# Decoder trunk on one core: convolution input kept in SBUF, attention loads moved to SP's queue, norm factors spread by PE transposes

## The chip, the cores and the metric

One core of a Trainium2 chip runs the whole program: two layers of a decoder trunk over 1024 tokens. The metric is device microseconds of one execution, the median of three runs. Matmuls run on TensorE (PE), element-wise work on VectorE (DVE), ScalarE (ACT) and GpSimd (POOL); SyncE (SP) only issues DMAs. POOL can issue DMAs too, on a queue of its own.

## The reference

```python
for i in range(DEPTH):                               # 2 layers, S = 1024 tokens, D_MODEL = 1024
    a = rmsnorm(h, norm_mix_pre[i])
    u = a @ w_in[i]                                   # q, k, v, qi, ki, wi, u_conv (512), u_pool (256)
    # partial rope on q, k, qi, ki
    y_attn = dsa_sparse_attention(q, k, v, qi, ki, wi)
    #   per block of 128 queries: index score of every causal key (16 heads), top 256 keys,
    #   softmax attention (8 heads of 64, 2 kv heads) over these keys alone
    y_conv = conformer_conv(u_conv, ...)
    #   y = a * sigmoid(g); causal depthwise conv, 31 taps; + bias; LayerNorm over 256; swish; 256x256
    y_pool = multiscale_pool(u_pool, ...)             # trailing means of 2/4/8/16, 64x64 maps, scale
    h = h + rmsnorm(concat(y_attn, y_conv, y_pool) @ w_out[i], norm_mix_post[i])
    m = square(relu(rmsnorm(h, norm_mlp_pre[i]) @ w_up[i])) @ w_down[i]       # d_ff = 4096
    h = h + rmsnorm(m, norm_mlp_post[i])
    h = h + sigmoid(h @ ple_gate[i]) * (p[i] @ ple_proj[i])
```

## The kernel before

Activations lie transposed: channels on the 128 lanes, tokens in the free dimension. Each layer is done in two halves of 512 tokens. The eight phases of `PHASES` alternate `win` (norm and the 21 units of the input projection) and `m` (output projection, MLP, gate) of (layer, half): win(0,0), win(0,1), m(0,0), win(1,0), m(0,1), win(1,1), m(1,0), m(1,1). A *unit* is one 128-channel output tile: 8 pieces of weights, each used in three 128x512 matmuls (lines 243, 248, 249) on a high and a low part of weights and activations.

**Weights** (`prepare`, line 196): SP loads 512 KB into one of two `wraw` buffers (line 199), ACT copies the high part into `whi` (line 204), POOL makes the low part `wlo` (line 205). `whi` and `wlo` have four tiles, two units' worth, so PE frees what ACT needs next.

**Background.** Convolution and pooling (`conv_pool`) and attention (`attention`) are Python generators. After every unit of a phase, `run` advances them by a share that `RATES` gives to the phase. A generator that has begun stays ahead of an attention that is inserted later (line 429). From the program so recorded a scheduler makes one fixed order for each engine's queue.

**Convolution input.** In `win_phase` the units A0, G0, A1, G1 give the gated input: DVE evacuates A into a `dtmp` tile (line 342), G is scaled, passes a tanh on ACT and is multiplied in (line 391); SP stores the tile to `cpS` in DRAM (line 392), as it does for the pooling input P0, P1 (line 397). `conv_pool` loads both back with their left context into `row` tiles (`window`, lines 475 and 477). Then DVE makes the 2 x 31 taps, one instruction each (lines 535 and 537), into a PSUM bank. The pooling has POOL adds (499 to 503), DVE means (508 to 510), a split (261) and three matmuls on `cmat`.

**Norm factors.** `token_sums` (line 298) makes sums over the lanes by matmuls with a column of ones; `rms` raises them to the power -1/2 on POOL (line 311); `spread` (line 303) copies four columns of factors over the lanes as four fp32 matmuls with `ident` as moving operand. This happens 16 times in `rms_sb` and `post_norm`, and in every `conv_pool` twice, for the mean (`mu`) and for the variance.

**Attention.** POOL issues the loads of keys `kd` (line 613), values `vst` (line 836), queries `qst` (line 608) and, at the start of an `m` phase, of the mixed heads `slot<-mixS` (line 923). The choice of 256 keys (`select`) is a search bit by bit: 31 rounds, in each of which ACT counts two blocks (line 683) and DVE two (line 669), with throw-away flags in tiles of the ring that is `spare`; in the second half of a layer that is the ring `row`, of which two tiles hold the packed scores. Buffers: `dtmp` 11, `row` 5 tiles.

## Time and profile before

| | us |
|---|---|
| median of 3 runs | 2843.78 (2837.95 to 2844.03) |
| profiled execution, own time | 2843.85 |
| its span, first to last instruction | 2842.1 |
| PE busy | 2720.5 (96%) |
| PE weight loads busy | 2242.8 (79%) |
| DVE busy | 1747.6 (61%) |
| ACT busy | 1548.1 (54%) |
| POOL busy | 1418.0 (50%) |
| granted TensorE clock, mean | 0.985 |

Busy time is the union of instruction times. Matmuls overlap: a 128x512 matmul is shown 0.39 us long, while the next one starts 0.23 us after it, so what a matmul costs is read from the distance of starts and not from its length. The profile's rows give start, length, engine, line, tiles and, in brackets, the idle time of the engine before and what ended it.

### The profile page before, as it was taken

Reading aid. Unit: us, or ns where it says so; the run is one execution under the profiler, and the core shown is the slowest. Engines: PE = TensorE matmul, PEld = TensorE weight load, DVE = VectorE, ACT = ScalarE, POOL = GpSimd, SP = SyncE. Lnnn points to the kernel's source line nnn. Section 1 sums busy time; section 2 is a strip of 40 time slices with the busy share of each in tenths; the row PEclk is TensorE's granted clock in tenths of the full one; section 3 lists DMA queues with packets and bytes.
Section 4 is the critical chain, followed back from the end, with each engine's and each line's share of the span. In section 5 each row is a group of like instructions: output and inputs, shape, how many; then the busy total and the mean of one; then the engine's idle time right before and its main releaser. Section 6 shows DMA issues by size and latency. Waiting matters only on the chain.

```text
span 2842.1 us, 37724 instructions
## 1 busy us (share of the span) xinstructions
PE 2720.5 (96%) x12648; PEld 2242.8 (79%) x12648; DVE 1747.6 (61%) x3473; ACT 1548.1 (54%) x2932; POOL 1418.0 (50%) x1161
## 2 busy tenths in 40 slices
PE   7899989999999999899999989999999999999998
PEld 6677777887888878778788777888878878788886
DVE  7969679788447775965822467587985561511123
ACT  5347667775567535766334423677757654533343
POOL 4655425444334665544544755444443356544446
PEclk9999999999999999999999999999999999999999
DMA  5676554422343576533333547534223354423233
GB/s 189 198 192 218 153 134 148 112 85 90 93 115 106 159 238 187 162 116 102 114 104 104 184 152 238 152 116 108 97 79 98 104 164 138 155 97 99 98 97 122
DMA packets 195666, 384.90 MB, mean 135 GB/s; under 512 B 17424, under 2 KB 76944, under 8 KB 195472
## 3 DMA queue, kind: packets, MB, share of 16 engines
q1 hardware_dynamic: 138192, 330.58, 35.7%
q0 software_dynamic: 57280, 51.91, 8.7%
q8 instruction: 100, 1.64, 0.3%
q14 instruction: 94, 0.77, 0.1%
HBM read 307.97 MB, written 74.45 MB: 135 GB/s over the span
## 4 chain that ended last, share of the span: by engine, by line
PE 72%; DVE 16%; DMA 5%; ACT 3%; issue 3%; POOL 1%; SPq 0%; POOLq 0%; DVEq 0%; ACTq 0%
PE pd L243 20%; PE pd L249 20%; PE pd L248 20%; PE bank L601 5%; DVE bank L537 2%; PE bank L789 2%; DVE dtmp L875 1%; DVE row L669 1%; DVE slot L261 1%; DMA row<-cpS 1%; PE bank L798 1%; PE bank L797 1%; DVE cmat L261 1%; PE pd L298 1%; DVE dtmp L261 1%
## 5 line engine op out<-in xcount | busy, mean ns | idle before, releaser
L205 POOL TENSOR_TENSOR wlo<-wraw,whi 128x512 fp32r<-128x512 f32 x824 | 1094.7, 1334 | 1180.6 <-ACT whi L204 1115.4
L243 PE MATMUL pd<-slot,whi 128*128 128x512 f32 x3296 | 1306.8, 397 | 50.7 <-DVE slot L261 14.5
L248 PE MATMUL pd<-slot,whi 128*128 128x512 f32 x3168 | 1246.0, 393 | 4.6 <-DVE slot L261 2.7
L249 PE MATMUL pd<-slot,wlo 128*128 128x512 f32 x3168 | 1241.9, 393 | 4.1 <-POOL wlo L205 4.0
L204 ACT ACTIVATE whi<-wraw 128x512 fp32r<-128x512 f32 x824 | 511.1, 627 | 731.3 <-PE pd L248 499.0
L243 PEld LDWEIGHTS pd<-slot,whi 128*128 128x128 f32 x3296 | 625.6, 190 | 188.4 <-DVE slot L261 16.6
L249 PEld LDWEIGHTS pd<-slot,wlo 128*128 128x128 f32 x3168 | 600.0, 189 | 130.9 <-POOL wlo L205 7.5
L248 PEld LDWEIGHTS pd<-slot,whi 128*128 128x128 f32 x3168 | 601.1, 190 | 125.8 <-DVE slot L266 3.9
L601 PE MATMUL bank<-kd,qst 128*128 128x512 f32 (+3 forms) x1024 | 261.5, 360 | 10.6 <-DVE mxc L767 3.7
L646 DVE SCALAR_TENSOR_TENSOR idx<-bank,wiT,idx 128x512 f32<-128x512 f32 (+3 forms) x300 | 189.3, 652 | 94.7 <-ACT bank L642 90.7
L601 PEld LDWEIGHTS bank<-kd,qst 128*128 128x128 f32 x1024 | 181.7, 192 | 46.6 <-DVE idx L646 6.8
L642 ACT ACTIVATE bank<-bank 128x512 f32<-128x512 f32 (+2 forms) x320 | 153.8, 506 | 90.0 <-PE bank L601 85.2
L981 DVE SCALAR_TENSOR_TENSOR pd<-pd,rb 128x512 f32<-128x512 f32 x112 | 77.7, 694 | 183.2 <-PE pd L249 183.2
L995 DVE TENSOR_TENSOR yT<-yT,pd 128x512 f32<-128x512 f32 x96 | 65.5, 684 | 197.8 <-PE pd L249 197.5
L537 DVE SCALAR_TENSOR_TENSOR bank<-row,vec,bank 128x512 f32<-128x512 f32 x232 | 162.1, 746 | 0.5
L669 DVE TENSOR_SCALAR_CACHE_REDUCE row<-row,cc 128x640 f32<-128x640 uint16 (+1 forms) x124 | 133.5, 1077 | 14.5 <-ACT row L683 12.6
L683 ACT ACTIVATE row<-row,cc 128x768 f32<-128x768 uint16 (+1 forms) x124 | 121.5, 983 | 18.0 <-DVE cc L689 15.3
L767 DVE CUSTOM_DVE_ANT_0 row<-bank,idx 128x512 f32<-128x512 f32 (+3 forms) x160 | 91.4, 591 | 64.0 <-PE bank L601 60.6
L261 DVE TENSOR_TENSOR cmat<-bank,cmat 128x512 fp32r<-128x512 f32 (+1 forms) x160 | 97.9, 631 | 49.4 <-ACT cmat L260 43.8
L261 DVE TENSOR_TENSOR slot<-pd,slot 128x512 fp32r<-128x512 f32 x112 | 76.6, 685 | 51.3 <-ACT slot L260 51.1
L982 ACT ACTIVATE pd<-pd 128x512 f32<-128x512 f32 x112 | 65.2, 582 | 72.8 <-DVE pd L981 72.7
L775 ACT ACTIVATE row<-row,nmc 128x384 f32<-128x384 f32 (+5 forms) x96 | 84.2, 878 | 27.8 <-DVE nmc L771 21.0
(216 smaller groups left out, 2828.7 us busy)
## 6 DMA issues: line engine op xcount, KB each, us to landing
wraw<-wup SPq DMA_DIRECT2D x128, 512.0 KB, 3.3
wraw<-wdown SPq DMA_DIRECT2D x128, 512.0 KB, 3.3
wraw<-win SPq DMA_DIRECT2D x84, 512.0 KB, 4.2
qiS<-dtmp SPq DMA_DIRECT2D x64, 256.0 KB, 2.5
slot<-mixS POOLq DMA_DIRECT2D x32, 512.0 KB, 7.0
wraw<-wgate SPq DMA_DIRECT2D x32, 512.0 KB, 3.6
qst<-qiS POOLq DMA_DIRECT2D x48, 256.0 KB, 3.7
hS<-yT SPq DMA_DIRECT2D x48, 256.0 KB, 3.6
```

What stands on the lines that cost most here:

```text
L204: sc.activation(hi, r, AF.Copy)
L205: gp.tensor_tensor(lo, r, hi.bitcast(F32), op=OP.subtract)
L243: te.matmul(ps, wh, xh, start=i == 0, stop=False)
L248: te.matmul(ps, wh, xl, start=False, stop=False)
L249: te.matmul(ps, wl, xh, start=False, stop=i == n - 1)
L261: ve.tensor_tensor(lo, src, hi.bitcast(F32), op=OP.subtract)
L537: ve.scalar_tensor_tensor(acc[:, c] if k == TAPS - 1 else pa, src, w, pa, op0=OP.mult, op1=OP.add)
L601: te.matmul(ps[:, :n1 - n0], q, kd[:, k, k0 + n0:k0 + n1], start=k == 0, stop=k == 1)
L642: sc.activation(r, r, AF.Relu)
L646: ve.scalar_tensor_tensor(at, r, w, at, op0=OP.mult, op1=OP.add)
L669: ve.tensor_scalar(flags[:, :Ws[j]], of[j], t, None, op0=op, op1=OP.add, accum_out=dst[:, j:j + 1])
L683: sc.activation(flags[:, :Ws[j]], of[j], AF.Sign, scale=-1.0, bias=c[:, j:j + 1], accum_out=cnt[:, j:j + 1])
```

## The change

- The gated convolution input is written into a tile of a new ring `win` (2 tiles of 2 x 542 columns, 30 of them left context). The context is zero in a layer's first half and is copied on ACT from the kept tile `halo` in the second. The store to `cpS`, the load back and two `dtmp` tiles per phase go; the pooling input still passes through DRAM (`plS`).
- Loads of `kd`, `vst` and `slot<-mixS` (16 pairs, 12 and 32 DMAs) are issued by SP instead of POOL. Those of `qst` stay on POOL.
- `spread` uses `te.transpose` instead of an fp32 matmul. The mean of the convolution's LayerNorm is one fp32 matmul with a 128x128 matrix of 1/256 in place of `token_sums`, a scaling and a `spread`.
- Rings: `dtmp` 11 to 9, `row` 5 to 4. Three of the eight `RATES` change.

```diff
-RATES = (1.171, 1.114, 0.558, 0.766, 0.722, 0.567, 0.741, 0.946)
+RATES = (1.205, 1.114, 0.558, 0.766, 0.751, 0.567, 0.731, 0.946)
...
-    dtmp = Ring("dtmp", 11, [P, HALF])
+    dtmp = Ring("dtmp", 9, [P, HALF])
...
-    rows = Ring("row", 5, [P, 1088])
+    rows = Ring("row", 4, [P, 1088])
+
+    wins = Ring("win", 2, [P, 2, TAPS - 1 + HALF])
+    halo = const.tile([P, 2, TAPS - 1], F32, name="halo")
...
-            te.matmul(ps[:, j * P:(j + 1) * P], t4[:, j:j + 1].to_broadcast([P, P]), ident, start=True, stop=True)
+            te.transpose(ps[:, j * P:(j + 1) * P], t4[:, j:j + 1].to_broadcast([P, P]), ident)
...
-                conv[name[1]] = evac(ps, half=True)
+                c = int(name[1])
+                if c == 0:
+                    yc = wins.get()
+                    if hf == 0:
+                        gp.memset(yc[:, :, :TAPS - 1], 0.0)
+                    else:
+                        sc.activation(yc[:, :, :TAPS - 1], halo, AF.Copy)
+                ve.scalar_tensor_tensor(yc[:, c, TAPS - 1:], ps, 0.5, rb, op0=OP.mult, op1=OP.mult)
...
-                y = conv[name[1]]
+                y = yc[:, c, TAPS - 1:]
                 ve.scalar_tensor_tensor(y, g, 1.0, y, op0=OP.add, op1=OP.mult)
-                sy.dma_start(cpS[l, c * P:(c + 1) * P, ts], y)
-                dtmp.put(y)
+                if c == 1 and hf == 0:
+
+                    sc.activation(halo, yc[:, :, HALF:], AF.Copy)
...
-        yt, yc = window(0, TAPS - 1)
...
-        token_sums(ps, [both])
+        te.matmul(ps, mean256, both, start=True, stop=True)
         ctmp.put(both)
-        mu = tiny("mu")
-        ve.tensor_scalar(mu, ps[:, :4], 1.0 / 256, None, op0=OP.mult)
-        spread(ps, mu)
...
-                gp.dma_start(kd[dup * 64:(dup + 1) * 64, :, k0:k0 + n],
+                sy.dma_start(kd[dup * 64:(dup + 1) * 64, :, k0:k0 + n].bitcast(F32),
...
-                            gp.dma_start(vst[:, v0:v0 + n // P], vS[l, bkv, :, :n // P])
+                            sy.dma_start(vst[:, v0:v0 + n // P].bitcast(F32), vS[l, bkv, :, :n // P])
...
-            gp.dma_start(xs[k], mixS[:, k * P:(k + 1) * P, ts].rearrange("k p t -> p k t"))
+            sy.dma_start(xs[k].bitcast(F32), mixS[:, k * P:(k + 1) * P, ts].rearrange("k p t -> p k t"))
```

The order of every queue moves with this. Line numbers of the changed kernel are 4 to 10 higher. First, DVE's queue in win(0,0), before. L535 and L537 are taps, `row_127` is the window loaded from `cpS`, L344 evacuates the pooling input P0 and then P1, L391 finishes G1:

```order
L349 TENSOR_TENSOR pd_138<-pd_138,rb_163 128x512
L391 SCALAR_TENSOR_TENSOR dtmp_107<-pd_138,dtmp_107 128x512
L344 TENSOR_TENSOR dtmp_103<-pd_139,rb_163 128x512
L535 TENSOR_SCALAR bank_142<-row_127,vec 128x512
L535 TENSOR_SCALAR bank_143<-row_127,vec 128x512
L537 SCALAR_TENSOR_TENSOR bank_142<-row_127,vec,bank_142 128x512
L344 TENSOR_TENSOR dtmp_104<-pd_137,rb_163 128x512
```

DVE's queue at the same place in the changed kernel; L401 finishes G0 and L395 begins A1, L545 and L547 are taps, L189 to L193 are rope tables:

```order
L401 SCALAR_TENSOR_TENSOR win_125<-pd_139,win_125 128x512
L190 TENSOR_SCALAR dtmp_104<-dtmp_101 128x512
L545 TENSOR_SCALAR bank_142<-win_125,vec 128x512
L191 TENSOR_SCALAR dtmp_104<-dtmp_104 128x512
L189 TENSOR_SCALAR dtmp_103<-dtmp_109,fr 128x512
L547 SCALAR_TENSOR_TENSOR bank_142<-win_125,vec,bank_142 128x512
L193 SCALAR_TENSOR_TENSOR dtmp_101<-dtmp_104,dtmp_101 128x512
L395 SCALAR_TENSOR_TENSOR win_125<-pd_137,rb_164 128x512
L547 SCALAR_TENSOR_TENSOR bank_142<-win_125,vec,bank_142 128x512
```

The first tap moves from behind G1 and P0 to right behind G0, and P1's evacuation has one load less in front of it that DVE must wait for.

Second, DVE's queue in a round of `select` of (0,1), before: L669 counts a block (640 and 1024 columns), its first name is the tile for the flags:

```order
L689 SCALAR_TENSOR_TENSOR cc_1427<-gec_1431,bank_141 128x4
L669 TENSOR_SCALAR row_125,cntc_1387<-row_126,cc_1427 128x640
L687 TENSOR_SCALAR bank_141<-cc_1427 128x4
L669 TENSOR_SCALAR row_127,cntc_1387<-row_124,cc_1427 128x1024
L688 TENSOR_TENSOR gec_1432<-cntc_1387,bank_141 128x4
L689 SCALAR_TENSOR_TENSOR cc_1428<-gec_1432,bank_141 128x4
L669 TENSOR_SCALAR row_127,cntc_1384<-row_126,cc_1428 128x640
```

The same in the changed kernel, where L676 counts:

```order
L696 SCALAR_TENSOR_TENSOR cc_1413<-gec_1421,bank_141 128x4
L694 TENSOR_SCALAR bank_141<-cc_1413 128x4
L676 TENSOR_SCALAR row_121,cntc_1373<-row_124,cc_1413 128x640
L676 TENSOR_SCALAR row_123,cntc_1373<-row_122,cc_1413 128x1024
L988 SCALAR_TENSOR_TENSOR pd_137<-pd_137,rb_164 128x512
L695 TENSOR_TENSOR gec_1418<-cntc_1373,bank_141 128x4
L696 SCALAR_TENSOR_TENSOR cc_1414<-gec_1418,bank_141 128x4
L694 TENSOR_SCALAR bank_141<-cc_1414 128x4
L676 TENSOR_SCALAR row_121,cntc_1374<-row_124,cc_1414 128x640
```

Two flag tiles (121 and 123) take the place of three (123, 125, 127), and an evacuation (L988) stands in the round.

Third, SP's queue in the changed kernel at the start of m(0,0); L819 stores a finished attention block, L620 and L843 load keys and values for the next half, L930 loads the mixed heads, L206 loads weights:

```order
L620 DMA kd<-kS 64x2x1024 x2
L819 DMA mixS<-ctmp_113 64x4x128
L819 DMA mixS<-ctmp_110 64x4x128
L843 DMA vst<-vS 128x1024
L819 DMA mixS<-ctmp_110 64x4x128
L819 DMA mixS<-ctmp_112 64x4x128
L930 DMA slot_75<-mixS 128x2x512
L930 DMA slot_76<-mixS 128x2x512
L930 DMA slot_77<-mixS 128x2x512
L930 DMA slot_78<-mixS 128x2x512
L206 DMA wraw_91<-wout 128x512
```

Before, SP's queue had only stores and weight loads here, and the four kinds of loads stood on POOL's.

## Rows read from the trace of the kernel before

**Rows 1.** The page, part 1: busy time and share of each engine.

```profile
PE 2720.5 (96%) x12648; PEld 2242.8 (79%) x12648; DVE 1747.6 (61%) x3473; ACT 1548.1 (54%) x2932; POOL 1418.0 (50%) x1161
```

**Rows 2.** Timeline of PE at 208: start, length, line, tiles, count.

```profile
208.46 0.39 PE L249 MATMUL pd<-slot,wlo 128*128 128x512 f32 x1
208.69 1.05 PE L303 MATMUL bank<-ident,muc 128*128 128x128 f32 x8
209.50 0.48 PE L243 MATMUL pd<-slot,whi 128*128 128x512 f32 x1
209.81 0.39 PE L248 MATMUL pd<-slot,whi 128*128 128x512 f32 x1
```

**Rows 3.** Timeline of PE at 741: twelve transposes of attention, line 789.

```profile
740.96 1.47 PE L789 MATMUL bank<-ident,row 128*128 128x128 f32 x12
742.19 0.48 PE L243 MATMUL pd<-slot,whi 128*128 128x512 f32 x1
```

**Rows 4.** Groups by line: PE's small norm matmuls of `conv_pool`.

```profile
L298 PE MATMUL bank<-ones,ctmp 128*128 128x1 f32 x64 | 7.6, 239 | 0.0
L303 PE MATMUL bank<-ident,muc 128*128 128x128 f32 x32 | 4.2, 274 | 0.0
```

**Rows 5.** Timeline of PE: the first matmuls on loaded `mixS`, m(0,0) and m(0,1).

```profile
389.55 0.50 PE L243 MATMUL pd<-slot,whi 128*128 128x512 f32 x1 [2.81 <-DMA slot<-mixS]
...
1095.70 0.47 PE L243 MATMUL pd<-slot,whi 128*128 128x512 f32 x1 [2.16 <-DMA slot<-mixS]
```

**Rows 6.** The page, part 6: DMA issues, KB each, median us to landing.

```profile
wraw<-wup SPq DMA_DIRECT2D x128, 512.0 KB, 3.3
slot<-mixS POOLq DMA_DIRECT2D x32, 512.0 KB, 7.0
```

**Rows 7.** Timeline of POOL's queue at the start of m(0,0).

```profile
384.02 2.81 POOL L923 DMA_DIRECT2D slot<-mixS  x4 [4.08 <-DMA mixS<-ctmp]
```

**Rows 8.** Waits of SP's queue, longest first in total: us, times, longest.

```profile
SPq L199 <- POOL wlo L205: 1677.3, 377, 20.5
```

**Rows 9.** Timeline of DVE, 58 to 62, in win(0,0): first taps.

```profile
58.80 1.53 DVE L535 TENSOR_SCALAR bank<-row,vec 128x512 f32<-128x512 f32 x2 [7.80 <-DMA row<-cpS]
61.49 4.69 DVE L537 SCALAR_TENSOR_TENSOR bank<-row,vec,bank 128x512 f32<-128x512 f32 x7
```

**Rows 10.** Timeline of PE: pooling matmuls in win(0,0), then win(1,1).

```profile
85.19 0.79 PE L243 MATMUL bank<-cmat,cmat 128*128 128x512 f32 x1 [5.30 <-ACT cmat L260]
...
1695.82 0.80 PE L248 MATMUL bank<-cmat,cmat 128*128 128x512 f32 x1 [5.44 <-DVE cmat L261]
```

**Rows 11.** Timeline of DVE at 1666, in win(1,1): first taps.

```profile
1666.27 1.53 DVE L535 TENSOR_SCALAR bank<-row,vec 128x512 f32<-128x512 f32 x2 [4.47 <-DMA row<-cpS]
```

**Rows 12.** Stretches of time: us, PE, PEld, DVE, ACT, POOL busy (count), granted clock, DMA share, GB/s.

```profile
70.00:105.00 35.00, 26.20 (x99) 20.39 (x97) 34.11 (x38) 8.70 (x15) 27.02 (x23) 0.85 0.52 144
...
1137.00:1220.00 83.00, 72.36 (x347) 59.08 (x345) 76.74 (x246) 65.35 (x161) 42.82 (x34) 0.96 0.48 145
```

**Rows 13.** Timeline of DVE, then ACT, in one round of `select` of (0,1).

```profile
556.16 0.16 DVE L689 SCALAR_TENSOR_TENSOR cc<-gec,bank 128x4 f32<-128x4 f32 x1
556.35 0.88 DVE L669 TENSOR_SCALAR_CACHE_REDUCE row<-row,cc 128x640 f32<-128x640 int16 x1
...
559.06 0.16 DVE L689 SCALAR_TENSOR_TENSOR cc<-gec,bank 128x4 f32<-128x4 f32 x1
...
556.41 0.94 ACT L683 ACTIVATE row<-row,cc 128x768 f32<-128x768 int16 x1 [0.33 <-DVE cc L689]
```

**Rows 14.** Timeline of PE behind `select`: (0,1), then (1,1).

```profile
685.41 0.79 PE L243 MATMUL pd<-slot,whi 128*128 128x512 f32 x1 [4.29 <-DVE slot L261]
...
2102.12 0.50 PE L243 MATMUL pd<-slot,whi 128*128 128x512 f32 x1 [3.99 <-DVE slot L261]
```

**Rows 15.** Timeline of SP's queue in the last `post_norm`.

```profile
2780.00 5.80 SPq L872 DMA_DIRECT2D dtmp<-hS  x3
2787.19 0.33 SPq L199 DMA_DIRECT2D wraw<-wgate  x1
```

More of the change, by code (lines that the diff above doesn't have):

```diff
@@ L116, in tile_trunk @@
     vS = dram.tile([DEPTH, 2, P, 8, P], F32, name="vS")
-    cpS = dram.tile([DEPTH, 512, S], F32, name="cpS")
+    plS = dram.tile([DEPTH, 256, S], F32, name="plS")
     eS = dram.tile([DEPTH, NK, P, S], F32, name="eS")
@@ L151, in tile_trunk @@
     sy.dma_start(cv, cinv)
-    jp = const.tile([P, P], F32, name="jp")
+    lent = dtmp.get()
+    jp = lent[:, :P]
     gp.iota(jp, pattern=[[1, P]], base=0, channel_multiplier=-1, allow_small_or_imprecise_dtypes=True)
@@ L157, in tile_trunk @@
     ve.memset(ones, 1.0)
+    mean256 = const.tile([P, P], F32, name="mean256")
+    ve.memset(mean256, 1.0 / 256)
     mhalf = const.tile([P, 4], F32, name="mhalf")
@@ L164, in tile_trunk @@
     ve.tensor_scalar(cbias[:, P:], jp, 0.0, -BIG, op0=OP.is_gt, op1=OP.mult)
+    dtmp.put(lent)
     wiT = const.tile([P, DEPTH, 8, 16], F32, name="wiT")
@@ L337, in table, with evac @@
             return out
-        def evac(ps, lanes=slice(0, P), half=False):
+        def evac(ps, lanes=slice(0, P)):
             x = dtmp.get()
-            if half:
-                ve.scalar_tensor_tensor(x[lanes], ps[lanes], 0.5, rb[lanes], op0=OP.mult, op1=OP.mult)
-            else:
-                ve.tensor_tensor(x[lanes], ps[lanes], rb[lanes], op=OP.mult)
+            ve.tensor_tensor(x[lanes], ps[lanes], rb[lanes], op=OP.mult)
             return x
@@ L377, in win_phase @@
         held = None
-        conv = {}
         for name in win_order(l, hf):
@@ L396, in win_phase @@
                 x = evac(ps)
-                sy.dma_start(cpS[l, 256 + c * P:256 + (c + 1) * P, ts], x)
+                sy.dma_start(plS[l, c * P:(c + 1) * P, ts], x)
                 dtmp.put(x)
                 if c == 1:
-                    bg.append(((l, hf), conv_pool(l, hf)))
+                    bg.append(((l, hf), conv_pool(l, hf, yc)))
             elif name in ("M0", "I0"):
@@ L451, in win_phase, with conv_pool @@
         rbs.put(rb)
-    def conv_pool(l, hf):
+    def conv_pool(l, hf, yc):
         t0 = hf * HALF
@@ L466, in small_weights, with window @@
             return (hi, lo), [(hi[:, j * P:(j + 1) * P], lo[:, j * P:(j + 1) * P]) for j in range(n)]
-        def window(r0, n):
+        def window(n):
             t = rows.get()
             x = t[:, :2 * (n + HALF)].rearrange("p (c t) -> p c t", c=2)
-            src = cpS[l, r0:r0 + 256].rearrange("(c p) t -> p c t", p=P)
+            src = plS[l].rearrange("(c p) t -> p c t", p=P)
             if hf == 0:
@@ L493, in conv_pool @@
         wt, cw = small_weights(0, 2)
-        pt_, pus = window(256, 15)
+        pt_, pus = window(15)
         for c in range(2):
@@ L540, in conv_pool @@
             banks.put(pa)
-        rows.put(yt)
+        wins.put(yc)
         while (l, hf) == (0, 0) and ("index", l, hf) not in state:
```

## The prediction

> **What bounds the kernel now.** I read first the engines' busy shares: PE is busy 96% of the span, the next engine 61% [rows 1]. So a microsecond leaves the kernel only where PE issues less, or where PE now stands idle: 2842.1 - 2720.5 = 121.6 us in all. What PE issues is read from the distance of starts in its timeline: dense 128x512 matmuls start 0.23 us apart [rows 2], so a unit of 24 of them takes 24 x 0.227 = 5.45 us. Then I read, stage by stage, what ended PE's idle time: the loads of the mixed heads [rows 5], the pooling's split in the `win` phases [rows 10], the split of attention behind `select` [rows 14], and the stretch in which convolution and the second `post_norm` share DVE [rows 12]. The change touches each of them. DVE, ACT and POOL count only through these waits.
>
> The sum starts from the profiled execution's own 2843.85 us, which is the median of the runs (2843.78) to 0.1 us. About 0.2%, 5.7 us, is what a measurement can tell from no change here.
>
> **1. PE's small matmuls.** One `spread` is four fp32 matmuls and appears as eight rows; from the first of them to the next dense matmul, and with the 0.08 us that this one's successor comes late, they cost (209.50 - 208.69) + 0.08 = 0.89 us, 0.11 a row [rows 2]. A transpose is one row: twelve cost (742.19 - 740.96) + 0.08 = 1.31 us, again 0.11 a row [rows 3]. So each kept `spread` falls from eight rows to four. There are 16 in `rms_sb` and `post_norm` and 4 for the variance: 20 x 4 x 0.11 = 8.8 us. The mean of the convolution is 64/4 = 16 rows of sums (half of the group's 64 belong to the variance: 32/4 = 8) and 32/4 = 8 rows of `spread` per half [rows 4]: 16 rows, 1.8 us. In its place stands one fp32 product of 512 columns, which the trace of before doesn't show. At least it is two rows at 0.227 = 0.45 us; at most four times the 128-column `spread` piece of two rows (4 x 0.22 = 0.89 us), or no gain at all (1.8). I take 0.89, since fp32 cost goes by columns in the nearest row; 4 x 0.9 = 3.6 us. Term: **-12.4** (from -14.2 to -8.8). The Trainium skill, FP8 and Floating Point Precision, section TensorE Precision Notes, says that true fp32 takes four passes; worked out at 0.227 us a pass that is an estimate of 0.91 us, and by it the sum stays; with a pass for a row, as the fp32 rows look in the timeline, it would be 0.4 us a half lower, 2825.7.
>
> **2. Loads of the mixed heads on SP.** PE waits for them at two places, 2.81 and 2.16 us [rows 5]. Landing takes a median of 7.0 us from POOL's queue, 3.3 for weights of the same 512 KB from SP's [rows 6]; POOL spends 0.70 us on issuing each, and its first load at that place had waited for the last stores of `mixS` [rows 7], a dependency that stays. With 3.7 us less of landing both waits could vanish (-5); if the loads share the transfer with weights as before, nothing is gained (0). I take **-3**. The Trainium skill, DMA: Bandwidth & Descriptors, section Issuing engines are not separate DMA queues, says that all issuing engines end on the same 16 DMA engines and that only the time to issue is saved. By that rule alone the gain is 0.70 - 0.33 = 0.4 us at each place, the term -0.8 and the sum 2 us higher; the two landing times in the page are the row against it, though they are not of the same stage.
>
> The loads of keys and values go to SP too, and there each stands ahead of the next weights. What is queued behind a waiting load is the weight stream. Its cover: SP itself waits 1677.3/377 = 4.4 us on average for a free `wraw` [rows 8], and two units' `whi` and `wlo` lie ahead, 2 x 5.45 us. I cost this at nothing; if the cover is gone, one load that waits 5 us longer than the 11 us of cover costs that rest. POOL loses 76 issues at 0.6 to 0.7 us, none of which ends a wait of PE outside the two above: nothing.
>
> **3. Convolution input in SBUF.** In win(0,0) DVE waits 7.80 us for the window from `cpS` and then makes taps at 4.69/7 = 0.67 us [rows 9]; in win(1,1) 4.47 us [rows 11]. In the changed queue the first tap stands right behind G0. That alone gives PE nothing, since PE waits not for taps but for the pooling's split: 5.30 and 5.44 us [rows 10]. By the order, 32 taps now stand on DVE ahead of the first split in win(0,0), 19 before: 13 x 0.67 = 8.7 us of added work against 7.8 of idle that goes. So the first wait stays as it is, and what is gained is that 13 taps are gone from behind it, where PE idles 35.00 - 26.20 = 8.8 us with DVE busy 34.11 of 35.00 at a mean granted clock of 0.85, between 2.4 and 1.2 GHz [rows 12]. Bounds: all of these 8.8 and the 5.44 of win(1,1), -14.2; or 0, if the taps fill DVE to the same point. I take **-6**, under half, since DVE stays full there.
>
> **4. conv(1,0) ahead of attention(1,0).** It has now begun before that attention is inserted, so it keeps priority and meets another part of m(0,1). Before, in the stretch 1137 to 1220, PE is idle 83.00 - 72.36 = 10.6 us while DVE is busy 76.74 [rows 12]. All of it can go (-10.6), or the convolution's DVE work lands next to the index scores, whose PSUM banks DVE frees (+5, half of it). I take **-4**.
>
> **5. dtmp 11 to 9.** `post_norm` reads residuals through what `dtmp` has left, now three tiles. In the last one three loads took 5.80 us before weights got their turn [rows 15], 1.9 us a tile. Two such places have no background to fill a gap (m(1,0)'s end and m(1,1)'s). One tile late at each: **+4** (from 0, if the loads are early enough, to 2 x 5.80 = +12).
>
> **6. row 5 to 4.** In the second halves `select` has two flag tiles for ACT's and DVE's counts. A round is now 559.06 - 556.16 = 2.90 us; DVE's first count begins 0.19 us after the threshold, beside ACT's, which begins at 0.25 and lasts 0.94 [rows 13]. With two tiles DVE's 640-column count uses the tile that ACT's count has just filled, so it begins after it: a round of about 2.90 + 1.1 to 1.2 us. 31 rounds in two halves at 1.15: +71 us on the chain of DVE and ACT. PE is covered by dense units: the changed order puts 31.25 units ahead of the first softmax scores where 24.4 (0,1) and 25.9 (1,1) stood: (6.85 + 5.35) x 5.45 = 66 us. The waits behind `select`, 4.29 and 3.99 us now [rows 14], so grow by 71 - 66 = **+5** (from 0 to +33 at 1.6 us a round, which is +99).
>
> Sum: -12.4 - 3 - 6 - 4 + 4 + 5 = -16.4; 2843.85 - 16.4 = **2827.5 us**.
>
> **The rivals.**
> - *A little, given back.* PE saves its rows (-12.4, or -8.8 at the low end), but the loads on SP are no faster, the convolution's taps only fill DVE earlier, conv(1,0) gains nothing, and dtmp and `select` cost their 4 and 5: about 2840 to 2844, within 0.2%. This is also the case that the change doesn't do in SBUF and on SP what it says. For it: DVE stays full in 70 to 105. Against it: three separate waits would all have to keep their length.
> - *DVE's stretches empty.* Terms 3 and 4 at their lower ends, the flag tiles covered: -12.4 - 3 - 14.2 - 10.6 + 4 + 0 = -36, 2808. For it: the low clock in 70 to 105 goes with the idle. Against it: the taps themselves remain.
> - *Slower: select is serialised.* The two flag tiles make ACT and DVE take turns on every count, and ACT has weight splits between its counts. At 1.6 us a round the term is +33 instead of +5: 2855. It decides from where terms 1 to 5 (-21.4) are eaten and 5.7 more: 66 + 27 = 93 us, 1.5 us a round. For it: the order's round shows the same two tiles in turn, and another evacuation on DVE inside the round. Against it: 12 units more stand on PE ahead of the scores in the two halves.
>
> **How the numbers follow.** Forecast (2815 to 2838) 0.47; a little, given back 0.17; DVE's stretches empty 0.16; slower 0.20. The range reaches from half of the third case to the slower one's price: 2806 to 2856. Faster by over 0.2%: 0.47 + 0.16 = 0.63; within: 0.17; slower: 0.20.
>
> **What would show it.** In the profile of after: `spread` with four rows and no eight; the product with `mean256` by the distance of starts around it (0.45, 0.89 or 1.8 us); the first tap behind G0; PE idle in the 35 us behind the first pooling split under 8.8; landing of `slot<-mixS` near 3.3 and PE's waits on it under 2; the distance of thresholds in `select` of (0,1) near 4.05 us and PE's waits behind it under 10; PE idle in the last `post_norm` no more than 2 us longer. Wrong would make it: rounds over 4.4 us, weights that come late behind loads on SP (PE waiting for `wlo`), or a stretch at 1.2 GHz that is new.

## The result, and the profile after

The changed kernel takes 2810.92 us (median of 4 runs, 2806.71 to 2815.9), the kernel before 2841.91 on the same chip: the ratio is 0.9893, 95% interval 0.9872 to 0.9914. That is 30.4 us of the 2843.8 of before (24 to 36); forecast were 16.4. The time lies in the whole range (2806 to 2856) but below the forecast's own part of it (2815 to 2838), near the price of the case *DVE's stretches empty* (2808), and the gain is nearly twice the forecast's. The profiled execution of after has a span of 2804.9 us; it is the fastest of its four, so its distance to the span of before, 37.2 us, is some 6 us more than the medians'.

The page, part 1, of after, as [rows 1]:

```profile
PE 2702.1 (96%) x12512; PEld 2229.0 (79%) x12512; DVE 1738.2 (62%) x3470; ACT 1553.9 (55%) x2936; POOL 1374.0 (49%) x1085
```

PE is still what sets the time. It has 136 rows less and is busy 18.4 us less, and its idle time fell from 121.6 to 2804.9 - 2702.1 = 102.8 us. So about half of the profile's gain is busy time and half is waiting, where the forecast put three quarters on PE's own rows.

PE's timeline of after: the fp32 product with `mean256` (L558) and a `spread` (L310), to be read like [rows 2]:

```profile
199.18 1.02 PE L558 MATMUL bank<-ctmp,mean 128*128 128x512 f32 x2
199.63 0.80 PE L256 MATMUL pd<-slot,wlo 128*128 128x512 f32 x1
200.27 0.40 PE L250 MATMUL pd<-slot,whi 128*128 128x512 f32 x1
...
214.19 0.60 PE L310 MATMUL bank<-ident,rrc 128*128 128x128 f32 x4
214.54 0.48 PE L255 MATMUL pd<-slot,whi 128*128 128x512 f32 x1
214.86 0.39 PE L256 MATMUL pd<-slot,wlo 128*128 128x512 f32 x1
```

A `spread` is four rows and costs (214.54 - 214.19) + 0.09 = 0.44 us, half of the 0.89 before. The mean's product is two rows; from 199.18 to 200.27 there lie 1.09 us, of which the dense row L256 is 0.23: 0.86 us, against 0.89 taken and 0.91 worked out from the Trainium skill's four passes.

PE's timeline of after at the waits that [rows 5, 10 and 14] show for before: the pooling and then the rope in win(0,0), the first matmul on loaded heads, behind `select` of (0,1), the rope in win(1,1), behind `select` of (1,1):

```profile
83.12 0.79 PE L250 MATMUL bank<-cmat,cmat 128*128 128x512 f32 x1 [2.97 <-ACT cmat L267]
...
100.21 0.79 PE L250 MATMUL pd<-slot,whi 128*128 128x512 f32 x1 [2.44 <-DVE dtmp L369]
...
377.94 0.80 PE L250 MATMUL pd<-slot,whi 128*128 128x512 f32 x1 [2.28 <-DMA slot<-mixS]
...
724.20 0.69 PE L608 MATMUL bank<-kd,qst 128*128 128x128 f32 x2 [6.84 <-DVE mxc L774]
...
1681.02 0.77 PE L250 MATMUL pd<-slot,whi 128*128 128x512 f32 x1 [4.68 <-DVE dtmp L369]
...
2102.15 0.69 PE L608 MATMUL bank<-kd,qst 128*128 128x128 f32 x2 [4.70 <-DVE mxc L774]
```

The pooling waits of 5.30 and 5.44 us became 2.97 and none; a wait for the rope is new in their place (2.44, 4.68). Of the two waits for `mixS` one is left. Behind `select` two waits of 4.29 and 3.99 on the dense side have become two of 6.84 and 4.70 on the scores.

The stretches of [rows 12] in after (us, PE, PEld, DVE, ACT, POOL busy, granted clock, DMA share, GB/s):

```profile
70.00:105.00 35.00, 28.16 (x106) 21.49 (x105) 34.16 (x49) 11.46 (x20) 25.23 (x20) 0.90 0.59 173
1137.00:1220.00 83.00, 77.79 (x360) 64.12 (x361) 68.59 (x135) 55.61 (x116) 46.21 (x39) 0.98 0.63 175
```

The first has 6.8 us of PE's idle time instead of 8.8, the second 5.2 instead of 10.6 (the same clock times, not the same work: after is some 11 to 15 us ahead there).

To see where the stalls went I summed, over PE's starts, the distance to the next start less the median distance of instructions of that line and shape. Rows that start late at the lower clock count in it too. That sum is 183.8 us in before and 159.5 in after. Up to the same dense matmul of the program (one of the three on each piece of weights is counted), after less before, in us (the sum of one kernel differs by some 3 us between profiles, as two kernels below show whose queues are still alike there):

| dense matmul, its time in before | stall, after less before |
|---|---|
| 192, 201.6 (win(0,0) done) | -2.9 |
| 448, 482.1 (attention (0,0) done, m(0,0) begun) | -6.0 |
| 704, 675.1 (`select` of (0,1)) | -8.4 |
| 1152, 1083.1 (win(1,0) done) | +5.6 |
| 1536, 1418.9 (m(0,1)'s attention and convolution done) | -12.5 |
| 1728, 1555.1 (m(0,1) nearly done) | -12.6 |
| 1984, 1767.9 (win(1,1)) | -23.7 |
| 2304, 2048.3 (`select` of (1,1)) | -22.8 |
| 3264, 2813.2 (end) | -24.3 |

Beside the 24.3 us of stalls, 11.9 us of PE's small work are gone. At the other end of the kernel nothing moved: over the last 120 us of before the two sums run side by side to 0.1 us.

### The profile page after: what moved, and what is told of

The parts are those of the page before. It is cut to its first block, busy times and chain, and to the rows that moved or that the text cites. A ratio compares the mean times of both kernels' runs of the same rounds, so it can differ in the third digit from the quotient of the medians.

```text
span 2804.9 us, 37372 instructions
## 1 busy us (share of the span) xinstructions
PE 2702.1 (96%) x12512; PEld 2229.0 (79%) x12512; DVE 1738.2 (62%) x3470; ACT 1553.9 (55%) x2936; POOL 1374.0 (49%) x1085
## 4 chain that ended last, share of the span: by engine, by line
PE 79%; DVE 12%; DMA 5%; issue 2%; ACT 2%; POOL 1%; SPq 0%; POOLq 0%; ACTq 0%; DVEq 0%
PE pd L250 23%; PE pd L256 22%; PE pd L255 22%; PE bank L608 6%; DVE bank L547 2%; PE bank L796 2%; PE bank L805 1%; PE bank L804 1%; DMA wraw<-win 1%; DVE dtmp L882 1%; DVE slot L268 1%; DVE row L759 1%; DVE slot L273 1%; PE pd L305 1%; DVE cmat L268 1%
## 5 line engine op out<-in xcount | busy, mean ns | idle before, releaser
L256 PE MATMUL pd<-slot,wlo 128*128 128x512 f32 x3168 | 1244.6, 394 | 1.4 <-POOL wlo L212 1.2
L256 PEld LDWEIGHTS pd<-slot,wlo 128*128 128x128 f32 x3168 | 600.4, 190 | 125.6 <-POOL wlo L212 2.5
L988 DVE SCALAR_TENSOR_TENSOR pd<-pd,rb 128x512 f32<-128x512 f32 x112 | 78.0, 696 | 163.8 <-PE pd L256 163.4
L676 DVE TENSOR_SCALAR_CACHE_REDUCE row<-row,cc 128x640 f32<-128x640 uint16 (+1 forms) x124 | 133.6, 1078 | 67.8 <-ACT row L690 60.5
L547 DVE SCALAR_TENSOR_TENSOR bank<-win,vec,bank 128x512 f32<-128x512 f32 x232 | 164.4, 746 | 1.1
L267 ACT ACTIVATE cmat<-bank 128x512 fp32r<-128x512 f32 (+1 forms) x160 | 83.5, 548 | 30.6 <-PE bank L796 26.9
```

Source lines behind the costliest of these rows:

```text
L256: te.matmul(ps, wl, xh, start=False, stop=i == n - 1)
L547: ve.scalar_tensor_tensor(acc[:, c] if k == TAPS - 1 else pa, src, w, pa, op0=OP.mult, op1=OP.add)
L676: ve.tensor_scalar(flags[:, :Ws[j]], of[j], t, None, op0=op, op1=OP.add, accum_out=dst[:, j:j + 1])
```

## The experiments

Each run is compared with the kernel before on its own chip; the us are (ratio - 1) x 2843.8. The intervals are some 3 to 6 us either way, that of a difference of two runs 4 to 7, so a smaller difference between two runs isn't told from none. First each part alone, and the changed kernel with the old rates.

**PE's part alone.** `spread` and the mean as in the diff; besides these only the place of two constant tiles changes:

```diff
-            te.matmul(ps[:, j * P:(j + 1) * P], t4[:, j:j + 1].to_broadcast([P, P]), ident, start=True, stop=True)
+            te.transpose(ps[:, j * P:(j + 1) * P], t4[:, j:j + 1].to_broadcast([P, P]), ident)
...
-        token_sums(ps, [both])
+        te.matmul(ps, mean256, both, start=True, stop=True)
...
-        mu = tiny("mu")
-        ve.tensor_scalar(mu, ps[:, :4], 1.0 / 256, None, op0=OP.mult)
-        spread(ps, mu)
```

> The kernel before with PE's part alone (spread by transposes, the mean as one fp32 product with a matrix of 1/256; rings, loads and rates as before). The prediction's step 1: -12.4 us, 2829.5 against 2842. Rival: the rows were issued in gaps where PE waits anyway, at most a third is gained: 2838 to 2842.

Measured: 0.9977 (0.9968 to 0.9986), -6.5 us. The rows are gained in full (13.7 us of small work), but 5 us of stalls came with them, 11 of them between 201 and 482 us and some given back later. PE's waits from 200 to 330, in this kernel and then in before (in total, times, longest):

```profile
PE bank L602 <- DVE mxc L768: 5.6, 3, 2.3
PE bank L790 <- DVE cc L690: 2.0, 1, 2.0
...
```

```profile
PE bank L601 <- DVE mxc L767: 2.5, 2, 1.7
PE bank L789 <- ACT ctmp L777: 0.7, 1, 0.7
...
```

Attention (0,0) stands elsewhere in the order and waits more: 5.6 instead of 2.5 us behind DVE for its scores. The other stalls of that stretch aren't told apart.

**The loads on SP alone.**

```diff
-                gp.dma_start(kd[dup * 64:(dup + 1) * 64, :, k0:k0 + n],
+                sy.dma_start(kd[dup * 64:(dup + 1) * 64, :, k0:k0 + n].bitcast(F32),
...
-                            gp.dma_start(vst[:, v0:v0 + n // P], vS[l, bkv, :, :n // P])
+                            sy.dma_start(vst[:, v0:v0 + n // P].bitcast(F32), vS[l, bkv, :, :n // P])
...
-            gp.dma_start(xs[k], mixS[:, k * P:(k + 1) * P, ts].rearrange("k p t -> p k t"))
+            sy.dma_start(xs[k].bitcast(F32), mixS[:, k * P:(k + 1) * P, ts].rearrange("k p t -> p k t"))
```

> The kernel before with the loads of keys, values and mixed heads on SP's queue, nothing else. The prediction's step 2: -3 us, 2839. Rival A: the 17 us that the forecast missed came from here (POOL relieved of 76 issues, earlier landing): 2825 to 2830. Rival B: weights come late behind loads: 2845 or more.

Measured: 0.9975 (0.9962 to 0.9988), -7.1 us (-11 to -3): above the forecast's 3, not the 17 of rival A.

**The convolution in SBUF alone**, with `dtmp` 9 and `row` 4.

```diff
-    dtmp = Ring("dtmp", 11, [P, HALF])
+    dtmp = Ring("dtmp", 9, [P, HALF])
...
-    rows = Ring("row", 5, [P, 1088])
+    rows = Ring("row", 4, [P, 1088])
...
+    wins = Ring("win", 2, [P, 2, TAPS - 1 + HALF])
...
-                sy.dma_start(cpS[l, c * P:(c + 1) * P, ts], y)
-                dtmp.put(y)
...
-        yt, yc = window(0, TAPS - 1)
...
```

> The kernel before with the convolution's input in SBUF alone, with the rings that this needs (dtmp 9, row 4), old loads, old rates. By the prediction's steps 3, 5, 6 with the old rates: -6 + 4 + 5 to +33, so 2845 to 2870. Theory after the result: the input's way through DRAM was mis-sized, this part alone carries some 17 us: 2825. Rival: the surplus comes from the rates, this part alone gives no gain: 2840 to 2846.

Measured: 0.9988 (0.9977 to 0.9998), -3.4 us. Its stalls against before are -0.4 us up to 202 us, so win(0,0) as a whole gained nothing; +2.2 at 1555 and -5.1 at 1768, so the gain is win(1,1)'s.

**The changed kernel with the old rates.**

```diff
-RATES = (1.205, 1.114, 0.558, 0.766, 0.751, 0.567, 0.731, 0.946)
+RATES = (1.171, 1.114, 0.558, 0.766, 0.722, 0.567, 0.741, 0.946)
```

> The changed kernel with the eight RATES of before. If the three rates only make up for the shorter background, 2811 to 2814. If the order that they set (dense units ahead of the softmax scores, convolution against the second post_norm) carries the surplus: 2825 or more.

Measured: 0.9893 (0.988 to 0.9905), -30.4 us: as the changed kernel. So no worth of the rates is seen, nor of the convolution (1,0) ahead of attention, which goes with them: its last taps begin at 1405.8 us in before, at 1399.0 here and at 1120.7 in the changed kernel. After's loss up to 1083 us and gain behind it in the table above are two sides of that. With the old rates the stalls are -1.5 us at 1083, -3.6 at 1419, -16.7 at the end.

The three parts alone add up to 17 us of 30. The next runs leave one out, two from the changed kernel and one built up from before; a fourth moves the rates alone.

**The changed kernel without SP's loads**: the three edits of the last diff, taken back.

> The changed kernel with the loads of keys, values and mixed heads back on POOL's queue. Alone on the kernel before the three parts gave -6.7 (PE), -7.4 (SP's loads) and -2.5 us (convolution in SBUF with its rings), 16.6 together, against 31 for the whole, so 14 us are gained only in company. If the loads are one half of a pair that works together (convolution's window gone from SP, loads gone from POOL), this run loses more than 7: 2825 to 2832. If each part only adds its own: 2818.

Measured: 0.9950 (0.9934 to 0.9965), -14.2 us: without SP's loads 16 us are lost.

**The changed kernel without PE's part:**

```diff
-            te.transpose(ps[:, j * P:(j + 1) * P], t4[:, j:j + 1].to_broadcast([P, P]), ident)
+            te.matmul(ps[:, j * P:(j + 1) * P], t4[:, j:j + 1].to_broadcast([P, P]), ident, start=True, stop=True)
...
-        te.matmul(ps, mean256, both, start=True, stop=True)
+        token_sums(ps, [both])
+        mu = tiny("mu")
+        ve.tensor_scalar(mu, ps[:, :4], 1.0 / 256, None, op0=OP.mult)
+        spread(ps, mu)
```

> The changed kernel with spread as fp32 matmuls and the mean by token_sums and spread, as before. If the rows count in full in the changed kernel (the prediction's 12.4 us; alone they gave 6.7, because waits of PE grew by 5 us): 2823 to 2825. If the parts only add: 2818. If it is the partner of the missing 14 us: 2831.

Measured: 0.9919 (0.9904 to 0.9934), -23.0: PE's part is worth 7 here, with an interval from 0 to 15.

**PE's part and SP's loads** on the kernel before, the first two diffs of this section together.

> The kernel before with PE's part and the loads on SP's queue, convolution still through DRAM, old rings and rates (the changed kernel without its SBUF part). By addition -14.1: 2830. If convolution is the partner of the missing 14 us, it stays there; if the pair PE and SP is what works together: 2816 to 2820.

Measured: 0.9935 (0.9919 to 0.995), -18.5: 5 us over the sum of the two, which isn't clear of none, and 12 short of the whole with the same old rates.

**The rates alone:**

```diff
-RATES = (1.171, 1.114, 0.558, 0.766, 0.722, 0.567, 0.741, 0.946)
+RATES = (1.205, 1.114, 0.558, 0.766, 0.751, 0.567, 0.731, 0.946)
```

> The kernel before with the three changed RATES alone: no instruction is added or removed, only the order of the queues moves. It shows what another order of the same work is worth by itself. Theory that order alone scatters the time: a difference of 3 to 10 us either way. Rival, that the order hardly matters: within 2 us of 2843.

Measured: 1.0044 (1.0029 to 1.006), +12.5. Same instructions, another order, and the largest loss that any one edit made from the kernel before. From one dense matmul of m(0,0) to the same last one of win(1,0), this kernel and then before:

```profile
860.50:1101.70 241.20, 227.41 (x1096) 188.55 (x1095) 189.01 (x297) 116.84 (x201) 143.51 (x118) 0.97 0.55 170
```

```profile
855.00:1083.00 228.00, 223.91 (x1119) 187.17 (x1118) 165.38 (x285) 119.18 (x207) 133.33 (x110) 1.00 0.56 170
```

The stretch is 13 us longer. PE idles 13.8 us instead of 4.1, and the granted clock is 0.97 instead of 1.00: 241 x 0.03 = 7 us more at most, an estimate from the mean clock. By the distances of starts, the rows that PE began while the clock was at the lower of its two levels (1.2 GHz) came 5.9 us late in all. One wait is the convolution's mean, whose `spread` PE reaches too early:

```profile
PE bank L303 <- DVE muc L551: 4.1, 1, 4.1
```

In the changed kernel that `spread` isn't there.

Then the two pairs that were missing with old rates, and the loads apart:

**Convolution in SBUF and SP's loads** on the kernel before, the two diffs together.

> The kernel before with the convolution in SBUF (dtmp 9, row 4) and the loads on SP's queue, PE's small matmuls and rates as before. By addition -3.4 - 7.1 = -10.5 us. If these two work together whatever the rates, as the changed kernel without PE's part says (ratio 0.9919): -20 to -24. If that pairing was the work of the new rates: -10.

Measured: 0.9931 (0.9917 to 0.9945), -19.6 us, 9 over the sum of the two alone (interval 3 to 15).

**Convolution in SBUF and PE's part** on the kernel before, the two diffs together.

> The kernel before with the convolution in SBUF (dtmp 9, row 4) and PE's part, loads on POOL's queue, old rates. By addition -10 us; the changed kernel without SP's loads gave a ratio of 0.9950, -14. If the mean granted clock is what is lost with the loads on POOL (0.982 in both kernels with the convolution in SBUF and loads on POOL), it is 0.982 to 0.983 here again.

Measured: 0.9931 (0.9913 to 0.9949), -19.6 us, 10 over the sum (3 to 16); the clock of the profiled run was 0.984, not 0.982 to 0.983.

**Keys and values back on POOL** in the changed kernel:

```diff
-                sy.dma_start(kd[dup * 64:(dup + 1) * 64, :, k0:k0 + n].bitcast(F32),
+                gp.dma_start(kd[dup * 64:(dup + 1) * 64, :, k0:k0 + n],
...
-                            sy.dma_start(vst[:, v0:v0 + n // P].bitcast(F32), vS[l, bkv, :, :n // P])
+                            gp.dma_start(vst[:, v0:v0 + n // P], vS[l, bkv, :, :n // P])
```

> The changed kernel with the loads of keys and values alone back on POOL's queue; the mixed heads stay on SP. Putting all three back cost 16 us. If what counts is POOL's queue standing behind loads that wait for PE to free kd and vst, with weights' low parts and query loads behind them, most of it is here: 2821 or more against 2811. If it is the mixed heads: 2811 to 2813.

Measured: 0.9934 (0.9921 to 0.9948), -18.8: 11.7 us of the 16 (5 to 19) lie in the loads of keys and values, whose issues the forecast had put at nothing.

**The mixed heads back on POOL** in the changed kernel:

```diff
-            sy.dma_start(xs[k].bitcast(F32), mixS[:, k * P:(k + 1) * P, ts].rearrange("k p t -> p k t"))
+            gp.dma_start(xs[k], mixS[:, k * P:(k + 1) * P, ts].rearrange("k p t -> p k t"))
```

> The changed kernel with the loads of the mixed heads alone back on POOL's queue. By the prediction's step 2 this is all of that step: +3 us, 2814. If the heads carry the 16 us: 2825. If keys and values do: no more than 2813.

Measured: 0.9908 (0.9892 to 0.9923), -26.2: 4.3 us, with an interval from -3 to +12. That is near the forecast's 3, and doesn't exclude nothing. That the two add up to the 16 of all three is closer than the intervals allow to read. Keys and values cost more than the heads: the two kernels ran on one chip, 7.4 us apart (2 to 13).

How keys on POOL cost PE time is seen in win(0,0). POOL's timeline with keys and values on POOL:

```profile
95.77 2.57 POOL L620 DMA_DIRECT2D kd<-kS  x4
98.33 1.31 POOL L342 TENSOR_TENSOR dtmp<-dtmp,rb 128x512 f32<-128x512 f32 x1
99.56 1.30 POOL L212 TENSOR_TENSOR wlo<-wraw,whi 128x512 fp32r<-128x512 f32 x1
100.78 1.29 POOL L342 TENSOR_TENSOR dtmp<-dtmp,rb 128x512 f32<-128x512 f32 x1
```

PE in that kernel:

```profile
105.16 0.80 PE L250 MATMUL pd<-slot,whi 128*128 128x512 f32 x1 [7.00 <-DVE dtmp L369]
...
155.06 3.35 PE L608 MATMUL bank<-kd,qst 128*128 128x384 f32 x10 [8.03 <-DMA qst<-qiS]
```

POOL in the changed kernel:

```profile
95.16 1.28 POOL L342 TENSOR_TENSOR dtmp<-dtmp,rb 128x512 f32<-128x512 f32 x1
96.40 1.73 POOL L212 TENSOR_TENSOR wlo<-wraw,whi 128x512 fp32r<-128x512 f32 x1
98.08 1.27 POOL L342 TENSOR_TENSOR dtmp<-dtmp,rb 128x512 f32<-128x512 f32 x1
```

PE there, at the same two places (the first stands above, 2.44 us):

```profile
151.54 3.46 PE L608 MATMUL bank<-kd,qst 128*128 128x384 f32 x10 [4.39 <-DMA qst<-qiS]
```

Four issues of 0.64 us stand ahead of two products with the norm factors (L342); DVE's rope (L368, L369) needs them, and PE needs the PSUM tile that DVE then frees. DVE with keys and values on POOL, then in the changed kernel:

```profile
100.25 0.68 DVE L368 TENSOR_TENSOR dtmp<-pd,dtmp 128x512 f32<-128x512 f32 x1
...
102.17 0.69 DVE L353 TENSOR_TENSOR pd<-pd,rb 128x512 f32<-128x512 f32 x1
...
104.43 0.68 DVE L369 TENSOR_TENSOR dtmp<-pd,dtmp 128x512 f32<-128x512 f32 x1
```

```profile
97.57 0.68 DVE L368 TENSOR_TENSOR dtmp<-pd,dtmp 128x512 f32<-128x512 f32 x1
...
99.48 0.68 DVE L369 TENSOR_TENSOR dtmp<-pd,dtmp 128x512 f32<-128x512 f32 x1
```

The second product ends 2.7 us later (102.07 instead of 99.35) and the rope's second part begins 4.95 us later: between the two stand an evacuation (L353), a split and a tap, which the order has there. So the issues (2.57 us) are a good half of the delay, and the order that comes with them is the rest.

The first wait is 7.00 instead of 2.44, 4.6 us. The second is 8.03 instead of 4.39, but the two differences don't add up, since at a place between them the changed kernel has the longer wait (first the changed kernel, then keys and values on POOL):

```profile
138.68 0.79 PE L250 MATMUL pd<-slot,whi 128*128 128x512 f32 x1 [3.98 <-DVE dtmp L268]
...
141.29 0.50 PE L250 MATMUL pd<-slot,whi 128*128 128x512 f32 x1 [0.82 <-DVE dtmp L268]
```

At the scores PE is 3.5 us behind (155.06 against 151.54), and 3.2 us at the end of win(0,0). The other kernels with the convolution in SBUF say the same of the first wait: with keys on POOL it is 6.95 us (the changed kernel without SP's loads), 7.04 (with PE's part) and 7.59 (the convolution alone); with keys on SP it is 2.33 to 2.44 in all seven. In before POOL issues the same four loads behind the two products, and PE has no such wait there: it is held by the pooling (POOL, then PE):

```profile
92.34 1.56 POOL L335 TENSOR_TENSOR dtmp<-dtmp,rb 128x512 f32<-128x512 f32 x1 [3.30 <-DVE dtmp L261]
...
95.11 1.29 POOL L335 TENSOR_TENSOR dtmp<-dtmp,rb 128x512 f32<-128x512 f32 x1
...
99.27 2.58 POOL L613 DMA_DIRECT2D kd<-kS  x4
...
100.27 0.80 PE L243 MATMUL bank<-cmat,cmat 128*128 128x512 f32 x1 [2.73 <-ACT cmat L260]
```

This is one part of what convolution and loads give only together. Up to 202 us the convolution changes the stalls by -0.4 us with the loads on POOL and by -4.0 with them on SP (-7.1 against -3.1); with PE's part by +1.8 and -2.9. So of the 9 us that convolution and loads gain over their sum, some 4 lie here, with the scatter of the table (3 us) on each figure.

A second place is small. With keys and values on POOL, PE waits at 1104.97 for a low part that stands behind two issues of values; without SP's loads the same wait is 1.63 us, and the changed kernel has none there (POOL, then PE):

```profile
1102.50 1.13 POOL L843 DMA_DIRECT2D vst<-vS  x2
1103.64 2.52 POOL L212 TENSOR_TENSOR wlo<-wraw,whi 128x512 fp32r<-128x512 f32 x2
...
1104.97 0.50 PE L256 MATMUL pd<-slot,wlo 128*128 128x512 f32 x1 [1.62 <-POOL wlo L212]
```

The rest of the 11.7 us isn't told apart by rows. At about 300 us the kernel with keys and values on POOL is 6.8 us of stalls behind the changed one, but the kernel with the heads alone on POOL, whose two waits are 2.38 and 5.24, is 8.6 behind there: what is lost after win(0,0) isn't shown to be the keys'.

Last, whether any new order costs the kernel before some us, and what the rings cost.

**The rings alone** on the kernel before:

```diff
-    dtmp = Ring("dtmp", 11, [P, HALF])
+    dtmp = Ring("dtmp", 9, [P, HALF])
...
-    rows = Ring("row", 5, [P, 1088])
+    rows = Ring("row", 4, [P, 1088])
```

> The kernel before with dtmp 9 and row 4 and nothing else: the flags of the search share two tiles, post_norm has three buffers, the convolution still goes through DRAM. The prediction's steps 5 and 6 at old rates: +4 and up to +12 us. The convolution in SBUF with these rings gave -3.4: if the rings cost 9, the convolution itself is worth 12; if they cost nothing, 3.

Measured: 1.0008 (0.9997 to 1.0019), +2.3 us, not clear of none. The round of `select` grew all the same. DVE and ACT in one round of (0,1) with four `row` tiles:

```profile
556.00 0.16 DVE L689 SCALAR_TENSOR_TENSOR cc<-gec,bank 128x4 f32<-128x4 f32 x1
557.68 0.88 DVE L669 TENSOR_SCALAR_CACHE_REDUCE row<-row,cc 128x640 f32<-128x640 int16 x1 [1.32 <-ACT row L683]
...
560.22 0.16 DVE L689 SCALAR_TENSOR_TENSOR cc<-gec,bank 128x4 f32<-128x4 f32 x1
...
556.63 0.92 ACT L683 ACTIVATE row<-row,cc 128x768 f32<-128x768 int16 x1
```

DVE waits for ACT's flags as forecast. Over the 31 rounds of (0,1) the mean distance of thresholds is 5.08 us here and 5.15 in the changed kernel, 3.90 before. So one round of 2.90 us, from which the prediction started, was shorter than before's mean by 1.0 us. The convolution itself is then worth -3.4 - 2.3 = -5.7 us alone, give or take 4. Of the two places where fewer tiles of `dtmp` were to make a load late, the end of m(1,0) has 1.3 us more stalls (2411 to 2468 us in before), the end of m(1,1) none.

**One rate at a time** on the kernel before, first the first:

```diff
-RATES = (1.171, 1.114, 0.558, 0.766, 0.722, 0.567, 0.741, 0.946)
+RATES = (1.205, 1.114, 0.558, 0.766, 0.722, 0.567, 0.741, 0.946)
```

> The kernel before with the first rate 1.205 in place of 1.171: same instructions, another order from the first phase on. If any new order costs the kernel before some us: +4 to +13. If a new order is as often better as worse, the three rates taken one by one give both signs.

Measured: 1.0012 (1.0001 to 1.0024), +3.4 us. It has the loss up to 1083 us (+15.3 us of stalls) and gives back 13 by 1419. This rate is the one that puts the convolution (1,0) ahead of attention: its last taps begin at 1136.1 us.

The fifth rate, from 0.722 to 0.751:

```diff
-RATES = (1.171, 1.114, 0.558, 0.766, 0.722, 0.567, 0.741, 0.946)
+RATES = (1.171, 1.114, 0.558, 0.766, 0.751, 0.567, 0.741, 0.946)
```

> The kernel before with the fifth rate 0.751 in place of 0.722: another order from m(0,1) on (about 1080 us). All three rates together lost 18 us up to there and gained 5 behind, so here -5 to 0; if any new order costs, +4 to +10.

Measured: 0.9997 (0.9987 to 1.0007), -0.9.

The seventh rate, from 0.741 to 0.731:

```diff
-RATES = (1.171, 1.114, 0.558, 0.766, 0.722, 0.567, 0.741, 0.946)
+RATES = (1.171, 1.114, 0.558, 0.766, 0.722, 0.567, 0.731, 0.946)
```

> The kernel before with the seventh rate 0.731 in place of 0.741: another order in m(1,0), the last with attention, alone. If any new order costs: +2 to +6; otherwise within 2 us.

Measured: 1.0017 (1.0006 to 1.0027), +4.8. So another order of the same work costs -1 to +5 us for one rate, +12.5 for three. That is not always a loss. Whether it is what the parts lack alone against what they are worth last (4 to 8 us, below) isn't shown. (The orders of these last two are as before's far beyond 600 us; their stalls at 584 us are 2.2 and 2.9 us below before's, which is the scatter of the table.)

**The queries on SP too**, in the changed kernel:

```diff
-            gp.dma_start(x, v[:, h0:h0 + 4, b * P:(b + 1) * P])
+            sy.dma_start(x.bitcast(F32), v[:, h0:h0 + 4, b * P:(b + 1) * P])
```

> The changed kernel with the loads of the queries (80, of 0.78 us each on POOL) on SP too. PE's waits on these loads are 6.5 us in the changed kernel, POOL stands 93 us behind PE for a free qst. If POOL's queue is the cost: -3 to -7, 2805. If SP now stands behind PE with the weights queued after it: +5 or more, with new waits on whi and wlo. No part of the computation changes.

Measured: 2810.73 us; ratio 0.9872 (0.9852 to 0.9892).

The same edit, with the rates of before:

> The same with the eight rates of before. The changed kernel with these rates took the same time as with its own, so the same sign as in the run above is expected if the queue is the cause: 2806 to 2809, or 2818 and more if SP's weights pay; different signs if it is the chance of one order.

Measured: 2809.09 us; ratio 0.9874 (0.9854 to 0.9894). The medians are those of the changed kernel (2810.92), the ratios lower because before ran at 2847.66 on that chip; the intervals overlap. That this beats the changed kernel isn't shown. The wait has only changed queues (waits of SP with queries on SP, then in the changed kernel):

```profile
SPq L206 <- POOL wlo L212: 1494.2, 369, 9.7
SPq L615 <- PE bank L608: 163.2, 45, 13.7
...
SPq L206 <- POOL wlo L212: 1623.1, 370, 16.4
```

SP stands 163 us behind PE, and has 129 us less to wait for weights' buffers: the cover of SP's slack holds, but PE's wait on queries is 8.5 us instead of 6.5.

## Why the prediction was wrong

**1, PE's rows: right.** Forecast -12.4, measured 11.9 us of small work in after (13.5 to 14.5 in the other kernels that have it); added last, the part is worth 10.8 us with old rates (-30.4 against -19.6) and 7.4 with the new ones. Alone it gave 6.5, since stalls came with it.

**2, loads: the step that failed is the sentence that costs POOL's 76 issues at nothing.** Putting keys and values alone back on POOL costs 11.7 us (5 to 19). Where it is seen, the four issues stand in POOL's queue ahead of the rope's products, and PE's wait behind DVE is 7.00 us instead of 2.44. I had looked only for PE's waits that name a load, and of the waits that name DVE I didn't ask which of them stood behind an issue of POOL; and I read that from before's order, where the pooling still hid this place. Of the 11.7 us some 3.5 are traced there and up to 1.6 behind an issue of values; the cause of the rest is open. The term for the mixed heads (-3) measured 4.3, which agrees, but its reason does not hold: their landing is 6.4 us on SP's queue, 7.0 before, and not the 3.3 of weights. So the landing agrees with the rule of the Trainium skill, DMA: Bandwidth & Descriptors, Issuing engines are not separate DMA queues, that I had weighed against it. What the same section calls usually small, the time to issue, is what counted here, by what stood behind it.

**3, convolution in SBUF: the number alone was luck, and in company it was short.** Forecast -6; alone -5.7 with the rings' cost taken out. But the term was to come in good part from win(0,0), and alone it gave nothing there (-0.4 us of stalls), while win(1,1) went to the upper end of the term's bounds: from 1555 to 1768 us the stalls of the four kernels with the convolution in SBUF that keep the old rates and have queries on POOL fall by 7.3 to 10.4 us, of the three without it that have PE's part, SP's loads or both by 2.9 to 5.0. The pooling's wait, which was to stay in win(0,0), fell from 5.30 to 2.97 us, and the rope's came behind it. Added last, with its rings, the part gives 12 us (-18.5 to -30.4).

**4, conv(1,0) ahead: forecast -4, measured 0.** In the kernel before, the first rate alone, which moves it, cost 3.4 us. The stretch that I priced did gain, but win(1,0), which I had not priced, lost as much (+15.3 us of stalls, then -13).

**5 and 6, rings: forecast +9, measured +2.3.** The search's rounds grew by 1.25 us (5.15 less 3.90, forecast 1.15), and the window of the 31 thresholds of (0,1) from 117 to 154 us. The size of that was right (31 x 1.25 = 39 us a half, forecast 36), though rounds over 4.4 us were my sign of being wrong: before's mean round was 3.90 and not the 2.90 of the one that I read. PE's waits behind `select` grew by 3 us (6.84 + 4.70 against 4.29 + 3.99), near the forecast's 5. `dtmp`, for which I had put 2 us at each of two places, cost at one. At the end of m(1,0) (2411 to 2468 us in before) the stalls rise by 4.2 us in the changed kernel and by 1.1 to 1.4 in the rings alone, the convolution alone and the changed kernel with old rates; in two kernels with eleven tiles they stay (+0.1 with the loads on SP, -0.2 with the seventh rate). At the end of m(1,1) PE's stalls are those of before, though the loads come as below, to be held against [rows 15]:

```profile
2743.98 5.36 SPq L879 DMA_DIRECT2D dtmp<-hS  x3
2750.74 0.33 SPq L206 DMA_DIRECT2D wraw<-wgate  x1
2751.29 6.33 SPq L879 DMA_DIRECT2D dtmp<-hS  x4
```

A round grew by less than the 1.5 us from which `select` would have decided.

The case *DVE's stretches empty*, whose price is nearest, is not what happened: conv(1,0) gave none of its 10.6 us, and the stretch from 70 to 105 still has 6.8 us of idle time.

With the terms as measured, -12 - 4.3 - 11.7 - 5.7 + 0 + 2.3 = -31.4, against 30.4 measured. That is 15 us below the forecast's -16.4; 11.7 of these are step 2's issues, the rest is smaller than the intervals. The agreement with the whole is better than the terms deserve: two of them are from the end of the change, two from its beginning. With old rates the parts give 6.5, 7.1 and 3.4 us as the first step and 10.8, 10.8 and 11.9 as the last one. One cause is shown with its place, the issues of the keys' loads on POOL ahead of the rope: they cost nothing as long as the pooling holds PE there, and some 4 us once it doesn't. Why PE's part brings 11 us of stalls into attention (0,0) when it is alone, 7 with SP's loads and none with the convolution in SBUF is open; the runs with other rates show that an order alone moved the sum that much (+15 us up to 1083).

## What to carry to other kernels

An issue of a DMA is an instruction of its engine's queue: cost it by what stands behind it there, down to the PSUM tile that someone frees late, and not by whether PE waits for its data. Price parts that touch one stage together, since the first one taken may only uncover the wait of the next; what a part is worth alone and what it is worth last differed here by a factor of about 1.5 to 3.5. And where a scheduler sets the order, run the same work in another order first: here three rates alone cost 12 us of 2844.

## What the runs showed of the hardware that I had not expected

A load of 512 KB on SP's queue isn't as fast as the weights on the same queue: the page, part 6, of after, us to landing:

```profile
wraw<-wup SPq DMA_DIRECT2D x128, 512.0 KB, 3.3
...
slot<-mixS SPq DMA_DIRECT2D x32, 512.0 KB, 6.4
```

From POOL's queue the heads took 7.0 us, so the queue changed little. Whether it is how they lie in DRAM or what runs beside them isn't shown. And the granted clock carries part of the price of an order: it is 1.00 up to the end of win(1,0) in before and 0.97 with the three new rates, where PE idled 9.7 us more; the rows begun at the lower level came 5.9 us late, on top of the idle time. The time to issue one load differed by what is loaded and by the engine: the heads took 0.73 us on POOL and 0.39 on SP, the keys 0.61 and 0.60 (medians of before and after).
